# GpSimd computes the low parts of sixteen weight tiles of the latent attention's gate, where VectorE did

## The chip, the cores and the metric

The kernel runs on one core of one Trainium2 chip, as one program. The metric is the device time of one execution in microseconds, taken as the median of several runs.

The core's engines each work through an instruction queue of their own, in order, and wait for each other through semaphores: TensorE (PE in the profile; its weight loads are PEld), VectorE (DVE), ScalarE (ACT), GpSimd (POOL) and SyncE (SP), which only issues transfers here.

## The reference

A stack of three blocks is computed in float32 for one sequence of 256 tokens of width 1024: a retention layer, a latent-attention layer (each followed by a small gated projection), and a block with a convolution, a pooling branch and a feed-forward part. The change touches the latent attention alone:

```python
z = h @ w_in                      # h: (1, 256, 1024)
c_q  = rms_norm(z[..., :768], q_norm_g)
c_kv = rms_norm(z[..., 768:1024], kv_norm_g)
k_rope = rope(z[..., 1024:1088], pos)
gate = z[..., 1088:]              # 2048 columns: 16 heads of 128
...                               # 16 heads of causal attention give o
return (jax.nn.silu(gate) * o) @ w_out
```

The gate's weights are the 2048 last columns of `w_in`, a matrix of 1024 x 2048 numbers.

## The kernel before

**Products in two parts.** A float32 matrix product is made of three products of a shorter format (float32r). Each operand is split into a high part (the operand rounded to that format) and a low part (what is left), and `mm` (L236) issues three matmuls for every 128x128 block of weights: high weights with high activations (L237), high weights with low activations (L238), low weights with high activations (L239). A product by `mm32` (L243) takes the operands whole, in one slower matmul.

**Weight tiles.** Weights arrive as tiles of 128 x 1024 numbers (512 KB), eight blocks of 128x128 in the order of use. `Seq.next` (L148) hands out one block, and calls `load` (L170) at the first block of a tile. `load` fetches the tile to a buffer `raw` (six buffers; the transfer is issued by SP, L165), ScalarE copies it to `wh`, the high part (L178), and VectorE subtracts that from the raw tile to get `wl`, the low part (L179). There are five buffers of `wh` and five of `wl`. A `raw` buffer is free again when both have read it; a `wh` and a `wl` buffer when TensorE has used its last block. So tiles are made ready ahead of TensorE, up to five at a time.

**Order.** The program is written in the order of TensorE's work. A planner puts every engine's instructions into one order when the kernel is built, by that order and by when their inputs should be ready; later that order is fixed. A small clock in the program (`after`, `every`, L203 and L423) delays pieces of work by a number of microseconds of TensorE's work, to give other engines time. One such piece is the modulation of the last block (`ada_steps`, L403): one chunk of 512 KB is fetched by SP, and VectorE multiplies and sums it (L413), every 7.61 us of that clock during this stage.

**The stage of the change.** TensorE's order in the latent attention is: three tiles for the rotary key and the latent key and value; six tiles for the latent query; the gate's products, sixteen tiles, two for each of the eight pairs of heads, by `mla_gate` (L822); and the pairs' projections, by `mla_proj` (L845). They are interleaved: six gate tiles (pairs 0 to 2), projections of pair 0, two gate tiles, projections of pair 1, four gate tiles, projections of pair 2, the last four gate tiles, projections of pair 3, and so on. Between them fall the sums of squares of the latent query (squares on ScalarE at L296, added on VectorE at L300 and L302, summed across partitions by TensorE at L363), from which `lora` (L778) makes the normalised latent query on VectorE and ScalarE (L783 to L793, with L187 and L188 for its two parts); the scores of each pair (L885 to L892); the softmax (L896 to L909 on VectorE, L901 and L902 on ScalarE); and the transposes of its result (L920). The result of a gate product leaves PSUM through VectorE (L831) and ScalarE (L832).

GpSimd does little in this kernel: some clearing of buffers, some transfers, and at the very end two additions (L1432).

The gate's sequence of tiles, which the change names, is made at L820:

```python
    seq_g = Seq(nouter("mla_in", range(16), range(8), 1088))
```

Of the kernel before, what the change touches and what calls it, by code (L numbers as in the profile page):

```python
# [11 lines left out]
F32 = mybir.dt.float32  # L12
# [7 lines left out]
P = 128  # L20
# [61 lines left out]
@with_exitstack  # L82
def tile_kernel(ctx, tc, order, xT, pT, pos, vec, cst, cv, rows, wada, wts, outT):
    nc = tc.nc
    V, A, T = nc.vector, nc.scalar, nc.tensor

    cp = ctx.enter_context(tc.tile_pool(name="cp", bufs=1))
    hp_ = ctx.enter_context(tc.tile_pool(name="half", bufs=14))
# [8 lines left out]
    def nm(s):  # L97
        uid[0] += 1
        return f"{s}_{uid[0]}"
# [7 lines left out]
    class Blk:  # L107

        def __init__(self, nb, dt=F32):
            self.t = [hp_.tile([P, 4, S], dt, tag="half", name=nm("half")) for _ in range((nb + 3) // 4)]  # L110
# [31 lines left out]


    class Seq:
        def __init__(self, entries, width=P, parts=True, ready=()):
            self.e, self.w, self.i, self.parts, self.ready = entries, width, 0, parts, list(ready)

        def next(self):  # L148
            per = D // self.w
            s = self.i % per  # L150
            if s == 0:
                self.h, self.l = load(self.e[self.i:self.i + per], self.w, self.parts, self.ready.pop(0) if self.ready else None)
            self.i += 1
            sl = slice(s * self.w, (s + 1) * self.w)
            return self.h[:, sl], self.l[:, sl]

    def fetch(entries, width, parts=True, step=D, pinned=False):
        g = len(order)
        order.append((width, list(entries)))
        n = len(entries) * width  # L160
        tag, bufs = (("raw", 6), ("wh", 5), ("wl", 5))[0 if parts else [0, 1][g % len([0, 1])]]
        raw = wp.tile([P, D], F32, tag=tag, name=nm("raw"), bufs=bufs)
        for o in range(0, n, step):
            e = min(n, o + step)
            d = nc.sync.dma_start(out=raw[:, o:e], in_=wts[g, :, o:e])  # L165
            if pinned:
                tc.keep_in_program_order(d)
        return raw[:, :n]

    def load(entries, width, parts=True, raw=None):  # L170
        if raw is None:
            raw = fetch(entries, width, parts)
        if not parts:
            return raw, raw
        n = raw.shape[1]
        hi = wp.tile([P, D], F32R, tag="wh", name=nm("wh"), bufs=5)[:, :n]
        lo = wp.tile([P, D], F32R, tag="wl", name=nm("wl"), bufs=5)[:, :n]
        A.copy(hi, raw)  # L178
        V.tensor_sub(lo, raw, hi.bitcast(F32))  # L179
        return hi, lo  # L180

    def nouter(name, ms, kbs, c0=0):
        return [(name, kb * P, c0 + m * P) for m in ms for kb in kbs]
# [247 lines left out]
    def ada():  # L431
        mods["n"] += 1
        next(ada_it, None)
# [383 lines left out]

    sgs = {}

    seq_g = Seq(nouter("mla_in", range(16), range(8), 1088))  # L820

    def mla_gate(p):  # L822

# [277 lines left out]
    def conv():  # L1101
        next(conv_it, None)
# [258 lines left out]

    late = late_steps()
    after(1.12, lambda: every(2.6, 3 * NA + 8, lambda: next(late)))


# [141 lines left out]
```

## Time and profile before

| What | Value |
|---|---|
| median of 3 runs | 845.04 us (843.58 to 845.37) |
| the profiled execution, its time | 842.56 us |
| its span in the profile | 840.8 us |
| TensorE busy | 823.7 us (98%) |
| VectorE busy | 702.4 us (84%) |
| ScalarE busy | 552.7 us (66%) |
| GpSimd busy | 9.9 us (1%) |
| subtractions at L179 | 233, 1222 ns each on average |

A row of a timeline gives the start from the beginning of the span, the duration, the engine, the line, the operation, what is written from what, the shape, and the count where neighbours are joined; what stands in brackets is how long the engine was idle before it and what it waited for. A row of the costliest groups ends with the busy time, the mean of one in ns, and the idle time before. `ps` is a tile in PSUM; the others (`t`, `half`, `raw`, `wh`, `wl`, `adach`, `siluc`) lie in SBUF. Busy time of TensorE includes matmuls that overlap.

### The profile page before, as it was taken

The numbers are of one execution on the slowest core, as the hardware profiler recorded it, in microseconds if no ns is written. First come the engines' busy times: TensorE is split into PE (matmuls) and PEld (weight loads), VectorE is DVE, ScalarE is ACT, GpSimd is POOL, SyncE is SP. The second block draws the span as 40 slices with busy tenths as digits, with TensorE's granted clock in tenths as the row PEclk, the third lists the DMA queues.
The fourth block names the chain that finished last, engine by engine and source line by source line (L and its number), as shares of the span: only waits on it lengthen the run. The fifth ranks groups of instructions, "written<-read, shape, count | busy, mean of one in ns | idle before, by whom it ended". The sixth has DMA issues, their size and how long they took to land.

```text
span 840.8 us, 15768 instructions
## 1 busy us (share of the span) xinstructions
PE 823.7 (98%) x6114; PEld 787.2 (94%) x6114; DVE 702.4 (84%) x1283; ACT 552.7 (66%) x966; POOL 9.9 (1%) x30
## 2 busy tenths in 40 slices
PE   8999999999999999998999999999999999999995
PEld 6989899999999999998999999899998999999885
DVE  6999798988889978688864767899677888889986
ACT  7655565555676787777754867998755576666551
POOL 0000000000000000000000000000000000000001
PEclk9999999999999999999999999999999999999999
DMA  9876567779556647364354355246363455567822
GB/s 333 330 253 221 206 225 273 253 267 323 174 176 249 250 149 255 135 242 150 109 181 176 118 209 176 76 174 196 132 240 113 148 188 191 179 220 252 274 79 76
DMA packets 46634, 167.48 MB, mean 199 GB/s; under 512 B 5216, under 2 KB 5472, under 8 KB 46560
## 3 DMA queue, kind: packets, MB, share of 16 engines
q1 hardware_dynamic: 45936, 164.38, 55.6%
q0 software_dynamic: 624, 2.10, 0.8%
q8 instruction: 48, 0.79, 0.4%
q14 instruction: 26, 0.21, 0.1%
HBM read 165.41 MB, written 1.05 MB: 198 GB/s over the span
## 4 chain that ended last, share of the span: by engine, by line
PE 51%; DVE 2%; ACT 1%; issue 1%; DVEq 0%
PE ps L238 13%; PE ps L237 13%; PE ps L239 13%; PE ps L243 10%; PE ps L341 1%; PE ps L363 0%; DVE wl L179 0%; PE ps L920 0%; PE ps L1170 0%; DVE t L1434 0%; DVE sm L1415 0%; DVE half L690 0%; DVE t L1411 0%; DVE t L1412 0%; PE ps L1407 0%
## 5 line engine op out<-in xcount | busy, mean ns | idle before, releaser
L237 PE MATMUL ps<-half,wh 128*128 128x256 f32 x1504 | 426.2, 284 | 0.0
L238 PE MATMUL ps<-half,wh 128*128 128x256 f32 x1504 | 424.0, 282 | 0.7 <-DVE half L188 0.6
L239 PE MATMUL ps<-half,wl 128*128 128x256 f32 x1504 | 422.2, 281 | 0.0
L178 ACT CAST wh<-raw 128x1024 fp32r<-128x1024 f32 x233 | 243.5, 1049 | 156.9 <-PE ps L238 99.7
L179 DVE TENSOR_TENSOR wl<-raw,wh 128x1024 fp32r<-128x1024 f32 x233 | 283.1, 1222 | 61.4 <-ACT wh L178 59.3
L238 PEld LDWEIGHTS ps<-half,wh 128*128 128x128 f32 x1504 | 283.6, 189 | 2.0 <-DVE half L188 1.1
L237 PEld LDWEIGHTS ps<-half,wh 128*128 128x128 f32 x1504 | 283.1, 188 | 1.1 <-ACT half L187 0.5
L239 PEld LDWEIGHTS ps<-half,wl 128*128 128x128 f32 x1504 | 284.0, 189 | 0.0
L243 PE MATMUL ps<-half,raw 128*128 128x256 f32 (+2 forms) x384 | 84.9, 380 | 0.0
L243 PEld LDWEIGHTS ps<-half,raw 128*128 128x128 f32 x384 | 72.6, 190 | 9.9
L237 PE MATMUL ps<-wh,half 128*128 128x512 f32 (+1 forms) x202 | 72.7, 361 | 1.0 <-ACT wh L178 1.0
L238 PE MATMUL ps<-wl,half 128*128 128x512 f32 (+1 forms) x202 | 71.1, 352 | 0.5 <-DVE wl L179 0.5
L239 PE MATMUL ps<-wh,half 128*128 128x512 f32 (+1 forms) x202 | 71.1, 352 | 0.0
L413 DVE CUSTOM_DVE_ANT_0 adach<-adach,siluc 128x1024 f32<-128x1024 f32 x48 | 58.6, 1222 | 13.8 <-DMA adach<-in_wada 13.8
L1087 ACT ACTIVATE t<-apad,vec 128x256 f32<-128x256 f32 x106 | 44.3, 500 | 0.5 <-DVE half L1088 0.5
L237 PEld LDWEIGHTS ps<-wh,half 128*128 128x128 f32 x202 | 38.0, 188 | 6.8 <-ACT wh L178 1.8
L238 PEld LDWEIGHTS ps<-wl,half 128*128 128x128 f32 x202 | 38.1, 189 | 6.0 <-DVE wl L179 1.0
L239 PEld LDWEIGHTS ps<-wh,half 128*128 128x128 f32 x202 | 38.0, 188 | 5.6
L1088 DVE TENSOR_TENSOR half<-half,t 128x512 f32<-128x512 f32 x53 | 36.6, 690 | 3.7 <-ACT t L1087 1.8
L187 ACT CAST half<-t 128x256 fp32r<-128x256 f32 (+1 forms) x47 | 20.6, 454 | 18.1 <-DVE t L1347 10.9
L188 DVE TENSOR_TENSOR half<-t,half 128x256 fp32r<-128x256 f32 (+1 forms) x47 | 21.8, 485 | 4.0 <-ACT half L187 3.0
L1342 ACT ACTIVATE t<-ps,vec 128x256 f32<-128x256 f32 x38 | 21.0, 557 | 2.0 <-PE ps L239 1.2
(290 smaller groups left out, 905.5 us busy)
## 6 DMA issues: line engine op xcount, KB each, us to landing
raw<-in_wts SPq DMA_DIRECT2D x257, 512.0 KB, 4.1
adach<-in_wada SPq DMA_DIRECT2D x48, 512.0 KB, 5.0
half<-in_xT SPq DMA_DIRECT2D x4, 256.0 KB, 6.0
half<-in_rows POOLq DMA_DIRECT2D x2, 512.0 KB, 4.5
out<-t SPq DMA_DIRECT2D x4, 256.0 KB, 2.0
cst<-in_cst SPq DMA_DIRECT2D x1, 928.0 KB, 10.6
raw<-in_wts SPq DMA_DIRECT2D x2, 256.0 KB, 4.2
siluc<-in_cv SPq DMA_DIRECT2D x1, 512.0 KB, 8.5
```

The source lines that it names most:

```text
L178: A.copy(hi, raw)
L179: V.tensor_sub(lo, raw, hi.bitcast(F32))
L187: A.copy(hi, src)
L188: V.tensor_sub(lo, src, hi.bitcast(F32))
L237: T.matmul(ps, l[0], r[0], start=first, stop=False)
L238: T.matmul(ps, l[0], r[1], start=False, stop=False)
L239: T.matmul(ps, l[1], r[0], start=False, stop=last)
L243: T.matmul(ps, w, r, start=first, stop=last)
L413: V.tensor_tensor_reduce(ch, ch, sc, 1.0, 0.0, MUL, ADD, mod[:, n:n + 1])
L1087: A.activation(t[:, b, :], apad[:, i0 + b, k:k + S], AF.Copy, scale=w[b])
L1088: V.tensor_add(acc.pair(i0 // 2), acc.pair(i0 // 2), t)
L1342: A.activation(t[:, b, :], ps[:, b, :], AF.Identity, bias=col("b_dw_f_2", m), scale=w[2])
```

## The change

`load` and `Seq` get an argument `by` with the engines for the two parts. The gate's sequence passes ScalarE for the high part, as before, and GpSimd for the low part. So sixteen of the 233 subtractions at L179 are issued to GpSimd's queue in place of VectorE's. All other sequences use the default, ScalarE and VectorE. The branch for a high part on GpSimd is not taken by any caller.

```diff
-    V, A, T = nc.vector, nc.scalar, nc.tensor
+    V, A, T, G = nc.vector, nc.scalar, nc.tensor, nc.gpsimd
...
-        def __init__(self, entries, width=P, parts=True, ready=()):
-            self.e, self.w, self.i, self.parts, self.ready = entries, width, 0, parts, list(ready)
+        def __init__(self, entries, width=P, parts=True, ready=(), by=None):
+            self.e, self.w, self.i, self.parts, self.ready, self.by = entries, width, 0, parts, list(ready), by
...
-                self.h, self.l = load(self.e[self.i:self.i + per], self.w, self.parts, self.ready.pop(0) if self.ready else None)
+                self.h, self.l = load(self.e[self.i:self.i + per], self.w, self.parts, self.ready.pop(0) if self.ready else None, self.by)
...
-    def load(entries, width, parts=True, raw=None):
+    def load(entries, width, parts=True, raw=None, by=None):
...
-        A.copy(hi, raw)
-        V.tensor_sub(lo, raw, hi.bitcast(F32))
+        first, second = by or (A, V)
+        if first is G:
+            G.tensor_copy(hi, raw)
+        else:
+            A.copy(hi, raw)
+        second.tensor_sub(lo, raw, hi.bitcast(F32))
...
-    seq_g = Seq(nouter("mla_in", range(16), range(8), 1088))
+    seq_g = Seq(nouter("mla_in", range(16), range(8), 1088), by=(A, G))
```

## Rows read from the trace of the kernel before

**Rows 1.** From the profile page: the first line of busy time, share and instructions by engine; the group of the subtractions at L179; and the group of the tile transfers, with its count, size and median time from issue to landing in us.

```profile
PE 823.7 (98%) x6114; PEld 787.2 (94%) x6114; DVE 702.4 (84%) x1283; ACT 552.7 (66%) x966; POOL 9.9 (1%) x30
...
L179 DVE TENSOR_TENSOR wl<-raw,wh 128x1024 fp32r<-128x1024 f32 x233 | 283.1, 1222 | 61.4 <-ACT wh L178 59.3
...
raw<-in_wts SPq DMA_DIRECT2D x257, 512.0 KB, 4.1
```

**Rows 2.** Busy time in three stretches of the stage of the change: the stretch, its length, then us and instructions of PE, PEld, DVE, ACT and POOL, the granted clock, the DMA share and GB/s. The last row is the same table for line L179 alone, where DVE is the only engine.

```profile
257.00:270.00 13.00, 13.00 (x112) 13.00 (x112) 12.32 (x22) 8.71 (x13) 0.00 (x0) 1.00 0.56 194
...
290.00:310.00 20.00, 19.04 (x158) 18.65 (x157) 14.64 (x39) 15.12 (x30) 0.00 (x0) 1.00 0.43 155
...
330.00:351.00 21.00, 21.00 (x177) 20.87 (x176) 14.80 (x34) 15.07 (x29) 0.00 (x0) 1.00 0.41 142
...
257.00:270.00 13.00, 6.22 (x6) 1.00 0.56 194
```

**Rows 3.** All waits of TensorE from 260 to 350 us (first row) and from 350 to 400 us (the others): who waited for whom, us in total, times, longest.

```profile
PE ps L920 <- DVE sm L909: 1.0, 1, 1.0
...
PE ps L920 <- DVE sm L909: 1.8, 1, 1.8
PE ps L243 <- ACT a L925: 0.7, 1, 0.7
```

**Rows 4.** GpSimd's two additions near the end: the timeline row of the first, then the summary of both (duration min/median/max in ns, start of the first and of the last in us); the same summary of VectorE's products at L1431 and of its operations at L1434, which read two tiles of SBUF.

```profile
831.77 1.73 POOL L1432 TENSOR_TENSOR t<-t,half 128x512 f32<-128x512 f32 x1 [12.68 <-DVE t L1431]
...
L1432 POOL TENSOR_TENSOR t<-t,half x2: 1252/1492/1732, 831.8 to 833.5; 128x512 f32<-128x512 f32 x2
...
L1431 DVE TENSOR_TENSOR t<-t,half x2: 683/688/693, 831.0 to 831.7; 128x512 f32<-128x512 f32 x2
...
L1434 DVE SCALAR_TENSOR_TENSOR t<-t,sm,half x2: 741/759/777, 834.5 to 835.3; 128x512 f32<-128x512 f32 x2
```

**Rows 5.** VectorE's timeline from the first gate tile's subtraction to the sixth's; the four between them and one accumulator read are left out, all else is there.

```profile
257.68 1.23 DVE L179 TENSOR_TENSOR wl<-raw,wh 128x1024 fp32r<-128x1024 f32 x1 [0.58 <-ACT wh L178]
258.83 0.86 DVE L188 TENSOR_TENSOR kr<-t,kr 64x256 fp32r<-64x256 f32 x2
259.72 0.42 DVE L367 TENSOR_TENSOR t<-t 128x256 f32<-128x256 f32 x1
...
261.20 0.42 DVE L372 SCALAR_TENSOR_TENSOR t<-t,t 128x256 f32<-128x256 f32 x1
261.53 1.22 DVE L413 CUSTOM_DVE_ANT_0 adach<-adach,siluc 128x1024 f32<-128x1024 f32 x1
...
262.68 0.42 DVE L373 SCALAR_TENSOR_TENSOR t<-t,t 128x256 f32<-128x256 f32 x1
263.01 0.68 DVE L300 TENSOR_TENSOR t<-t,t 128x512 f32<-128x512 f32 x1
263.62 0.42 DVE L789 TENSOR_TENSOR t<-t,t 128x256 f32<-128x256 f32 x1
...
265.09 0.87 DVE L792 SCALAR_TENSOR_TENSOR t<-ps,gq,t 128x256 f32<-128x256 f32 x2
...
267.01 0.75 DVE L188 TENSOR_TENSOR half<-t,half 128x256 fp32r<-128x256 f32 x2
...
268.81 0.68 DVE L300 TENSOR_TENSOR t<-t,t 128x512 f32<-128x512 f32 x1
269.53 0.43 DVE L302 TENSOR_TENSOR t<-t 128x256 f32<-128x256 f32 x1
269.87 1.22 DVE L179 TENSOR_TENSOR wl<-raw,wh 128x1024 fp32r<-128x1024 f32 x1
```

**Rows 6.** ScalarE's cast of the first gate tile, and from TensorE's timeline the first use of that tile's low part, the sum over the squares of the latent query, and the first use of the sixth gate tile's low part.

```profile
256.60 1.05 ACT L178 CAST wh<-raw 128x1024 fp32r<-128x1024 f32 x1
...
266.16 0.28 PE L239 MATMUL ps<-half,wl 128*128 128x256 f32 x1
...
270.15 0.59 PE L363 MATMUL ps<-t,ones 128*128 128x256 f32 x2
...
280.78 0.28 PE L239 MATMUL ps<-half,wl 128*128 128x256 f32 x1
```

**Rows 7.** Timeline rows around later points: the fetch that follows the first gate tile's subtraction and the cast of the tile it brought; VectorE's low parts of the first pair's keys and values, and the first matmul of its scores; the casts of the ninth and tenth gate tile, and the first use of the ninth's low part; the cast of the last gate tile, and the first use of its low part.

```profile
258.94 0.33 SPq L165 DMA_DIRECT2D raw<-in_wts  x1
...
271.93 1.03 ACT L178 CAST wh<-raw 128x1024 fp32r<-128x1024 f32 x1
...
293.33 1.02 DVE L188 TENSOR_TENSOR t<-ps,t 128x512 fp32r<-128x512 f32 x2
...
295.85 0.28 PE L237 MATMUL ps<-kr,t 128*128 128x256 f32 x1
...
307.94 2.02 ACT L178 CAST wh<-raw 128x1024 fp32r<-128x1024 f32 x2
...
311.61 0.28 PE L239 MATMUL ps<-half,wl 128*128 128x256 f32 x1
...
345.26 1.05 ACT L178 CAST wh<-raw 128x1024 fp32r<-128x1024 f32 x1 [0.41 <-ACT sm L902]
...
348.45 0.40 PE L239 MATMUL ps<-half,wl 128*128 128x256 f32 x2
```

## The prediction

> **What bounds the kernel now.** I began with busy time by engine. TensorE is busy for 823.7 of the 840.8 us of the span and VectorE for 702.4 [rows 1]. That is an average, so next I cut the stage of the change, from 257 us (the first gate tile) to 351 us (the last), into stretches. TensorE is without a gap at the start and at the end; between 290 and 310 us it has 19.04 of 20.00. VectorE is nearly as full at the start, 12.32 of 13.00 from 257 to 270 us, and has room at the end, 14.80 of 21.00 [rows 2]. The waits of TensorE put a price on what a freer VectorE could give back: between 260 and 350 us it waits once, for 1.0 us, for the softmax's last scaling (L909). After 350 us the two waits are 1.8 and 0.7 us [rows 3]. So the stage is bound by TensorE, VectorE close behind it, and a gain is capped at about 1.0 us there. The change can cost more than it can give, if VectorE or the tiles come late.
>
> **What is moved.** Sixteen subtractions of 128x1024 at L179, 1222 ns each on average [rows 1], leave VectorE. Each held its queue for 1.14 us, since the next instruction starts about 0.08 us before it ends. That frees 16 x 1.14 = 18.2 us of VectorE, 5.7 of them with the first five gate tiles, in the full stretch (L179 takes 6.22 us there, gate tiles alone) [rows 2]. The first-part casts on ScalarE, all matmuls and all transfers keep their number.
>
> **What GpSimd pays.** The trace has this kind of operation only at half the size: two 128x512 additions (L1432), 1732 and 1252 ns [rows 4]. Doubling the faster gives 2.50 us as an upper end without disturbance, 1.25 us (no growth) is the lower. VectorE's own two-input operation goes from 688 ns at 512 columns (L1431) to 1222 at 1024 [rows 1, 4], a factor of 1.78; I take 1.25 x 1.78 = 2.22 us. Six gate tiles in a row are needed by TensorE every 2.8 us (first uses of the low part from 266.16 to 280.78 us) [rows 6], so GpSimd alone keeps pace. It can also start early: the first cast ends at 257.65, and the tile is wanted at 266.16 [rows 6]. Six at 2.22 us end at about 271, against a last need of 280.78. Later tiles have less room: the cast of one ends near 308.99 and its low part is used at 311.61 (2.62 us later), that of the last ends at 346.31 and is used at 348.45 (2.14 us) [rows 7]. At 2.22 us that is a stall of 0 and 0.1.
>
> **The queue of transfers.** A raw buffer is released by the subtraction: the fetch at 258.94 us follows the end of the first gate tile's at 258.91 [rows 5, 7]. A later end delays that fetch and the modulation chunks queued behind it on SP. The fetched tile is the sixth after it, cast at 271.93; landing takes 4.1 us [rows 1, 7], so it was there at 263.0 and 8.9 us are spare. Nothing else stands on GpSimd's queue in this stage. I cost this edit at zero; a delay of over 8.9 us would expose it.
>
> **The disputed cost: do the two engines exclude each other?** The first of the two additions on GpSimd started at 831.77, while VectorE ran its second L1431 (from 831.7, 0.69 us long, so until 832.4), and took 0.48 us longer than the second, which had no such neighbour [rows 4]. The excess is about what was left of VectorE's operation (0.6). Both read two operands from SBUF. I read this as one port, held by one of them at a time. It shows GpSimd waiting; no row shows VectorE waiting for GpSimd. The bounds are therefore zero (VectorE never waits) and the whole of each subtraction. I take the whole, because exclusion that is real for one side is most simply mutual, and because whoever comes second finds it taken.
>
> The Trainium skill says the same of the other direction, and speaks against this change: in "SBUF — State Buffer", section "Who interferes with whom", "A DVE instruction with two SBUF inputs contends with a GpSimd instruction that reads SBUF", and the second to issue is blocked until the first finishes. The row agrees for GpSimd as the loser (0.48 us); no run here yet shows VectorE as the loser. By that rule the sum is the one below, while a reading of the row in which only GpSimd waits gives the second rival.
>
> **The sum.** From 257.65 us VectorE's work up to the end of L302 is, without gate tiles: kr parts 0.86, L367 0.42, L372 0.42, L413 1.22, L373 0.42, L300 0.68, L789 0.42, half parts 0.75, L300 0.68, L302 0.43, together 6.30 us, less nine overlaps of 0.08, 5.6 us [rows 5]. All have two SBUF operands; only L792 (0.87) reads PSUM and can run beside GpSimd. Five subtractions fall before L302: 5 x 2.22 = 11.1. One port needs 16.7 us for both, so L302 ends at 274.35. It ended at 269.96, and TensorE used its sum at 270.15 (L363) [rows 5, 6]: 0.19 spare. Late by 274.35 - 269.96 - 0.19 = 4.2 us. TensorE's order is fixed, so everything behind L363 waits too, and a latent chain that follows on VectorE (normalise, split, the query projection) stays as late. The break-even price of a subtraction is (12.31 + 0.19 - 5.6) / 5 = 1.38 us.
> A second place is the first head pair's key split, done at 294.35 and used by the scores from 295.85 [rows 7], 1.5 us spare. Two gate tiles lie before it: 2 x 2.22 of blocking less 2 x 1.14 of relief is 2.2, so 0.7 remains. The last tile's 0.1 is added. The remaining eight lie where VectorE has gaps or reads PSUM, and I give them zero (up to 1.5 in all). Sum: 4.2 + 0.7 + 0.1 = 5.0 us. On the profiled execution that is 842.56 + 5.0 = 847.6. That execution is 2.5 us under the median of the runs (845.04), so the forecast is 850.0 us.
> Its own ends: at 1.25 us a tile nothing is late (845); at 2.50 us L302 is late by 5.6, by 8.1 if the sixth subtraction also gets in ahead of it, and with 2 us for the later groups 10 us, 855.
>
> **The rivals.**
> First, not slower: VectorE never waits for GpSimd, and TensorE's order covers the rest. For it: the 7 to 10 us of lead of the first six tiles, and L1434 on VectorE at 834.50, which started within the second addition (833.50 to 834.72) and took only 0.04 us over its like [rows 4]. That row is weak, as it overlaps only the tail. Price: -0.5 to +0.5, so 845. It decides if a subtraction holds VectorE for under 1.38 us.
> Second, GpSimd alone is the loser: each subtraction is stretched as the first addition was, to 2 x 1.73 = 3.46 us, VectorE runs on. The six still make it (257.65 + 20.8 = 278.4, before 280.78); the tile at 308.99 is late by 0.84 and the last by 1.32: +2.2, 847.2.
> Third, faster: the relief pulls the softmax scaling forward, so that the 1.0 us wait and the 1.8 us one after 350 go: 845.04 - 2.8 = 842.2. Against it: VectorE has gaps before both (14.64 of 20.00 from 290 to 310 us, 14.80 of 21.00 from 330) [rows 2], so it isn't a queue that makes them late, and the gate tiles are over by 350.
>
> **How the numbers follow.** What a measurement of this kernel can tell from no change is about 0.2%, 1.7 us. The forecast gets 0.45, nearly all of it slower. The first rival 0.28, nearly all within 0.2%. The second 0.17, three quarters of it slower. The third 0.10, faster. Slower: 0.44 + 0.13 + 0.01 = 0.58; faster: 0.10 + 0.02 = 0.12; same 0.30. The range goes from 843.0, which leaves out most of the third rival, to 855.0, the upper end of the forecast's bounds. The forecast's own range is 847 to 855.
>
> **What the profile afterwards would show.** Sixteen subtractions on GpSimd near 2.2 us if undisturbed, longer if it waits. If the port is shared as I think, VectorE's two-operand instructions of 0.4 to 1.2 us that meet a subtraction are stretched by up to 2.2 us, while those that read PSUM are not, and TensorE waits for some 4 us at L363 near 270 us. If that wait isn't there and VectorE's durations are unchanged, the first or second rival holds. A wait of TensorE at L239 for the low part from GpSimd speaks for the second. Wrong altogether would be an operation of GpSimd above 5 us, which makes even the first six late, or a re-ordering of TensorE's instructions that covers the lateness with other matmuls.

## The result and the profile after

The changed kernel takes 855.7 us (median of 4 runs, 853.63 to 856.93), the kernel before, with its runs beside them, 844.31 (843.35 to 845.37). The ratio is 1.0135, with a 95% interval from 1.0116 to 1.0155: slower by 11.4 us. The direction was as forecast; the size was not (850.0, range 843.0 to 855.0). The profiled execution took 855.21 us with a span of 853.4 us, 12.65 us more than the profiled one of before, so the steps below add up to 12.65.

The page of the changed kernel (most of its lines stand five lower in the code: the cast is L183, the subtraction L184) shows that the change does what it says [rows 1]:

```profile
PE 829.5 (97%) x6114; PEld 791.7 (93%) x6114; DVE 703.1 (82%) x1267; ACT 551.2 (65%) x966; POOL 50.5 (6%) x46
...
L184 POOL TENSOR_TENSOR wl<-raw,wh 128x1024 fp32r<-128x1024 f32 x16 | 40.5, 2556 | 162.1 <-ACT wh L183 150.4
```

Sixteen subtractions moved, and VectorE is nevertheless as busy as it was. Sixteen times 1.22 us went away, and about as much came back in instructions that last longer. TensorE has the same 6114 matmuls.

All waits of TensorE from 240 to 370 us (who waited for whom, us in total, times, longest) [rows 3]:

```profile
PE ps L368 <- DVE t L307: 5.5, 1, 5.5
PE ps L926 <- DVE sm L915: 3.1, 1, 3.1
PE ps L244 <- POOL wl L184: 0.4, 1, 0.4
```

The first is the wait that the forecast named (the sum of squares, L363 before). The second, for the softmax, was 1.0 us before. For GpSimd's own product TensorE waits 0.4 us in all.

Busy time in stretches, with the granted clock in the third number from the end [rows 2]; of the stretches of 2 us, the first two lie in and behind the first wait, the last behind the second:

```profile
257.00:270.00 13.00, 13.00 (x113) 13.00 (x112) 11.92 (x14) 5.84 (x10) 7.47 (x3) 1.00 0.43 153
270.00:290.00 20.00, 14.45 (x107) 14.06 (x107) 15.56 (x25) 10.52 (x17) 7.59 (x3) 0.83 0.51 184
...
310.00:330.00 20.00, 16.90 (x128) 16.57 (x127) 11.94 (x26) 14.77 (x29) 10.09 (x4) 0.91 0.46 165
...
274.00:276.00 2.00, 0.00 (x0) 0.00 (x1) 1.95 (x1) 0.00 (x0) 2.00 (x2) 0.50 0.65 244
276.00:278.00 2.00, 2.00 (x7) 1.82 (x8) 0.42 (x1) 0.22 (x1) 2.00 (x1) 0.50 0.61 186
...
318.00:320.00 2.00, 2.00 (x12) 2.00 (x11) 1.36 (x5) 2.00 (x5) 1.33 (x1) 0.50 0.35 74
```

From 257 to 270 us VectorE is "busy" for 11.92 us with 14 instructions; before it did 22 in 12.32 [rows 2]. From 274 to 276 TensorE does nothing. When it goes on, its granted clock is 0.50, the lower level (1.2 GHz), and it gets 7 matmuls into 2 us, where 19 are usual. The 12 from 318 to 320 are the same picture behind the second wait.

What VectorE did in that time, and GpSimd beside it (timelines) [rows 5]:

```profile
258.17 5.02 DVE L193 TENSOR_TENSOR kr<-t,kr 64x256 fp32r<-64x256 f32 x2 [0.91 <-ACT kr L192]
263.22 2.52 DVE L372 TENSOR_TENSOR t<-t 128x256 f32<-128x256 f32 x1
265.77 0.43 DVE L377 SCALAR_TENSOR_TENSOR t<-t,t 128x256 f32<-128x256 f32 x1
...
271.96 1.50 DVE L305 TENSOR_TENSOR t<-t,t 128x512 f32<-128x512 f32 x1 [1.65 <-ACT t L301]
273.50 2.44 DVE L307 TENSOR_TENSOR t<-t 128x256 f32<-128x256 f32 x1
277.26 0.42 DVE L789 SCALAR_TENSOR_TENSOR t<-ps,nr 128x256 f32<-128x256 f32 x1 [1.31 <-PE ps L368]
...
298.97 2.60 DVE L765 TENSOR_TENSOR t<-t,t 128x256 f32<-128x256 f32 x1
...
306.39 1.23 DVE L184 TENSOR_TENSOR wl<-raw,wh 128x1024 fp32r<-128x1024 f32 x1 [1.39 <-ACT wh L183]
...
313.18 1.22 DVE L418 CUSTOM_DVE_ANT_0 adach<-adach,siluc 128x1024 f32<-128x1024 f32 x1 [2.60 <-DMA adach<-in_wada]
```

```profile
257.98 7.47 POOL L184 TENSOR_TENSOR wl<-raw,wh 128x1024 fp32r<-128x1024 f32 x3 [100.83 <-ACT wh L183]
270.57 7.59 POOL L184 TENSOR_TENSOR wl<-raw,wh 128x1024 fp32r<-128x1024 f32 x3 [5.13 <-ACT wh L183]
295.45 5.83 POOL L184 TENSOR_TENSOR wl<-raw,wh 128x1024 fp32r<-128x1024 f32 x2 [17.28 <-ACT wh L183]
```

The two instructions for `kr` took 0.86 us before and take 5.02; L372 took 0.42 and takes 2.52 [rows 5]. The three end one after the other with the three subtractions between 257.98 and 265.45, each about 0.3 us behind the end of one. L377 starts when they are over and takes 0.43. L789, which reads PSUM, runs within the second group (270.57 to 278.16) and takes 0.42. So VectorE is held for up to 2.1 us at a time by a subtraction already under way; the held instructions have both of their operands in SBUF, the one that reads PSUM is not held.

Then the queue of transfers: SP's issues (the duration spans the joined issues with the waits between), and SP's waits for subtractions from 255 to 320 us, two rows after the change and one before it [rows 7].

```profile
260.40 15.62 SPq L165 DMA_DIRECT2D raw<-in_wts  x5
276.07 0.42 SPq L411 DMA_DIRECT2D adach<-in_wada  x1
...
307.64 0.33 SPq L165 DMA_DIRECT2D raw<-in_wts  x1
308.02 0.73 SPq L411 DMA_DIRECT2D adach<-in_wada  x1
```

```profile
SPq L165 <- POOL wl L184: 26.4, 8, 7.1
SPq L165 <- DVE wl L184: 9.9, 4, 5.5
...
SPq L165 <- DVE wl L179: 22.0, 10, 5.1
```

SP waits 26.4 us for GpSimd's subtractions to free their raw buffers, but it waited 22.0 us for VectorE's before: it runs ahead and waits in either kernel, so the length of its waits says little. What counts is when a fetch goes out. Before, the chunk of the modulation behind the same five weight fetches went out at 269.30 us; now it goes at 276.07, behind a fetch that waited for GpSimd. The one at 308.02 is the chunk for which VectorE waits 2.60 us ahead of the softmax (L418 at 313.18). It went out at 297.97 before, so it is 10.05 us late where the scores of the first pair are 7.46 us late. The fetch in front of it (307.64) went out 0.02 us after the end of one of VectorE's own subtractions (306.39 to 307.62). By the rows that one was late because VectorE had been held at L765 by GpSimd's second subtraction of the third group, ScalarE had waited 3.87 us for L765, and the cast that the subtraction needs stands behind that on ScalarE. So in this place it is the held VectorE, and not GpSimd's own subtraction, that frees the raw buffer late.

The scores of a pair (first matmul `ps<-kr,t`) serve as marks for the lag, which is how much later than in the kernel before TensorE reaches the same matmul. In the changed kernel, first, second and eighth pair:

```profile
303.31 0.28 PE L242 MATMUL ps<-kr,t 128*128 128x256 f32 x1
...
326.02 0.28 PE L242 MATMUL ps<-kr,t 128*128 128x256 f32 x1
...
433.23 0.28 PE L242 MATMUL ps<-kr,t 128*128 128x256 f32 x1
```

and in the kernel before, second and eighth (the first is in [rows 7]; the fourth pair starts at 377.31 after the change and at 365.44 before):

```profile
315.02 0.28 PE L237 MATMUL ps<-kr,t 128*128 128x256 f32 x1
...
420.60 0.28 PE L237 MATMUL ps<-kr,t 128*128 128x256 f32 x1
```

The lag is 303.31 - 295.85 = 7.46 us at the first pair, then 11.00 at the second, 11.87 at the fourth and 12.63 at the eighth. It comes in two jumps, at the two waits, and 1.6 us trickle in later. At the sum itself the lag is 276.00 - 270.15 = 5.85; the other 1.6 of the first jump is gathered behind it, where TensorE waits for nothing and runs at the lower clock. The second jump is 3.5: 2.1 us more wait at the softmax, and 1.4 behind it.

A lag counts from the beginning of the span, so it also holds what an execution lost ahead of this stage. A mark for that is the previous sum of squares, the last one before the first gate tile: it starts at 252.00 us in the kernel before and at 252.14 after the change (0.14 us of lag), but up to 3.2 us late in the runs below that leave the chunks on SP. Where that matters, the lag from this mark on is given too.

```profile
252.00 0.60 PE L363 MATMUL ps<-t,ones 128*128 128x256 f32 x2
```

### The profile page after: what moved, and what is told of

Its sections match the earlier page's. It is cut to its first block, busy times and chain, and to the rows that moved or that the text cites. A ratio compares the mean times of both kernels' runs of the same rounds, so it can differ in the third digit from the quotient of the medians.

```text
span 853.4 us, 15781 instructions
## 1 busy us (share of the span) xinstructions
PE 829.5 (97%) x6114; PEld 791.7 (93%) x6114; DVE 703.1 (82%) x1267; ACT 551.2 (65%) x966; POOL 50.5 (6%) x46
## 4 chain that ended last, share of the span: by engine, by line
PE 40%; DVE 8%; DMA 3%; issue 2%; ACT 1%; DVEq 0%; SPq 0%; POOLq 0%
PE ps L243 10%; PE ps L242 10%; PE ps L248 10%; PE ps L244 10%; DVE wl L184 2%; DMA adach<-in_wada 1%; DMA g<-mod 1%; PE ps L346 1%; DVE t L1317 1%; DMA half<-g 1%; PE ps L368 0%; DVE t L1349 0%; DVE half L193 0%; DVE t L1350 0%; DVE sm L1421 0%
## 5 line engine op out<-in xcount | busy, mean ns | idle before, releaser
L183 ACT CAST wh<-raw 128x1024 fp32r<-128x1024 f32 x233 | 243.4, 1048 | 147.7 <-PE ps L243 94.2
L184 DVE TENSOR_TENSOR wl<-raw,wh 128x1024 fp32r<-128x1024 f32 x217 | 263.2, 1220 | 57.2 <-ACT wh L183 55.3
L418 DVE CUSTOM_DVE_ANT_0 adach<-adach,siluc 128x1024 f32<-128x1024 f32 x48 | 58.5, 1220 | 15.7 <-DMA adach<-in_wada 15.6
L184 POOL TENSOR_TENSOR wl<-raw,wh 128x1024 fp32r<-128x1024 f32 x16 | 40.5, 2556 | 162.1 <-ACT wh L183 150.4
## 6 DMA issues: line engine op xcount, KB each, us to landing
cst<-in_cst SPq DMA_DIRECT2D x1, 928.0 KB, 10.6
```

Of the source, the lines that this page charges most:

```text
L184: second.tensor_sub(lo, raw, hi.bitcast(F32))
L418: V.tensor_tensor_reduce(ch, ch, sc, 1.0, 0.0, MUL, ADD, mod[:, n:n + 1])
```

## The experiments

Theory A became, in the course of the runs: two causes. GpSimd's subtraction, reading SBUF, holds VectorE's two-operand instructions; and a late subtraction (GpSimd's own, or one of VectorE's behind a held instruction) keeps a raw buffer, so that SP's queue, with the modulation chunk in it, is late and VectorE, in order, waits for the chunk. Both make TensorE stand, and it then runs at the lower clock for some us. Theory B, the rival, has the held VectorE alone.

**Halves of the change.** Low parts on GpSimd for the first six gate tiles only, for the last ten only, and for tiles 8 to 11 only (counted from 0). Of the last the idea was that there GpSimd meets work with PSUM operands.

```diff
-                self.h, self.l = load(..., self.by)
+                self.h, self.l = load(..., self.by if self.i // per < 6 else None)
```

(`>= 6` in the second, `8 <= self.i // per < 12` in the third.)

> Only the first six gate tiles' low parts go to GpSimd, the other ten stay on VectorE. Theory A (GpSimd and VectorE exclude each other while both read two operands from SBUF, in both directions): TensorE waits 5 to 6 us at the sum over the squares of the latent query, then runs some 3 us at the lower clock, and nothing else is lost: 7 to 8 us slower than before, 852. Rival B (the low parts simply come late, VectorE is not held): the six are wanted 7 to 10 us after their casts, so nothing waits, within 1 us of before. Rival C (the planner's new order costs the time, wherever the tiles are computed): a loss without VectorE's instructions being longer.

> The other half: gate tiles seven to sixteen on GpSimd, the first six on VectorE. Theory A: no wait at the sum over the squares, the wait at the transposes of the first pair (3.1 us in the changed kernel against 1.0 before) and the lower clock behind it stay, and so do the small losses at the last tiles: 3 to 6 us slower than before, 848 to 850, so that this and the run with the first six add up to about 12. Rival B: the ninth and the last tile late, 1 to 2 us. Rival C: no forecast.

> Only gate tiles nine to twelve on GpSimd, where VectorE's neighbouring work reads PSUM or has room. Theory A: nothing late, within 1.5 us of before (844), a place without cost but with nothing to gain, since TensorE doesn't wait there. Rival H (each subtraction moved to GpSimd costs its share, wherever it stands): four sixteenths of 11.4 us, 847.

Measured: first six 852.93 us, 1.0096 [1.0075, 1.0117]; last ten 850.12, 1.0068 [1.0053, 1.0083]; four tiles 845.26, 1.0014 [0.9995, 1.0032]. With the first six TensorE waits 5.5 us for the sum, as in the full change, and 1.0 for the softmax, as before; the lag is 7.46 at the first scores and 7.37 at the last. With the last ten there is no wait for the sum, and 3.5 us for the softmax. So the two jumps have separate origins, and the first six tiles carry the larger part. In the run with the first six the second jump is absent; the chunk that goes out at 308.02 in the full change goes out at 305.43 there, 7.46 us later than before, which is just the lag of the scores. The halves add up to 8.1 + 5.7 = 13.8 us (the ratio less one, times the 844.4 us of before), against 11.4. The second wait is 3.1 in the full change, not 3.5; the rest of the difference is not explained, and is about what the intervals of the three runs leave open. The four tiles cost nothing that can be measured, and gain nothing: TensorE has no wait there to give back.

**Hold or absence?** VectorE makes every low part, and GpSimd does the same subtraction once more into the raw tile, which nobody reads afterwards.

```diff
-        second.tensor_sub(lo, raw, hi.bitcast(F32))
+        V.tensor_sub(lo, raw, hi.bitcast(F32))
+        if second is G:
+            G.tensor_sub(raw, raw, hi.bitcast(F32))
```

> VectorE makes all low parts as before, and GpSimd repeats the sixteen subtractions, writing into the raw tile that nobody reads any more. No instruction of TensorE waits for GpSimd's results. Theory A: VectorE is held by the sixteen and not relieved of any: at least as slow as the changed kernel, 856 to 875, with VectorE's two-operand instructions stretched to 2.4 us. Rival B: only the raw and high-part buffers come free later: 844 to 847.

And GpSimd only writes: it clears both tiles before ScalarE and VectorE fill them.

```diff
+        if second is G:
+            G.memset(hi.bitcast(F32), 0.0)
+            G.memset(lo.bitcast(F32), 0.0)
...
-        second.tensor_sub(lo, raw, hi.bitcast(F32))
+        V.tensor_sub(lo, raw, hi.bitcast(F32))
```

> VectorE makes all low parts as before; GpSimd clears the high and the low buffer of each of the sixteen gate tiles before the cast and the subtraction fill them: the same engine, the same places, some 2 us of work per tile that writes SBUF and reads nothing. Theory A (the excluded thing is reading): no VectorE instruction is stretched, within 2 us of before (the cast waits for the clearing, with room for it). Rival D (any work of GpSimd on SBUF holds VectorE, or the semaphores between the three engines cost it): 5 us or more slower, with stretched VectorE instructions.

Measured: doubled 864.77 us, 1.0241 [1.0226, 1.0256]; write-only 847.31, 1.0041 [1.0015, 1.0067]. TensorE's wait for the sum with the doubled work; then, with the clearing, a row of VectorE's timeline and GpSimd beside it:

```profile
PE ps L370 <- DVE t L309: 9.8, 1, 9.8
```

```profile
264.27 0.68 DVE L308 TENSOR_TENSOR t<-t,t 128x512 f32<-128x512 f32 x1
...
264.03 0.95 POOL L184 MEMSET wh<- 128x1024 f32 x1 [0.98 <-PE ps L246]
```

With no relief for VectorE the wait grows from 5.5 to 9.8: the presence of GpSimd's subtraction costs, not the lateness of its product. GpSimd clears for most of 255.59 to 271.55 us, in pairs of 0.95 us each with pauses of 1 us. The addition of the squares (L308, both operands in SBUF) lies wholly inside one clearing and takes 0.68, as before; beside a subtraction, in the changed kernel, it took 1.50 (L305). So GpSimd's writing alone did not hold it. The Trainium skill states this in "SBUF — State Buffer", section "Who interferes with whom": VectorE with two SBUF operands contends with a GpSimd instruction that reads SBUF, "not with one that only writes it". Both halves of that sentence agree with these rows (1.50 us beside a subtraction, 0.68 beside a clearing). The time of this run is 2.9 us above the kernel before, where at most 2 were expected. Nothing of it stands at the sum (271.34 less the mark at 253.19 is 18.15 us, as it was before); it comes later, and what causes it was not separated.

**Shorter holds.** Each of GpSimd's subtractions is cut into four of 256 columns.

```diff
-        second.tensor_sub(lo, raw, hi.bitcast(F32))
+        for o in range(0, n, 256 if second is G else n):
+            e = o + (256 if second is G else n)
+            second.tensor_sub(lo[:, o:e], raw[:, o:e], hi[:, o:e].bitcast(F32))
```

> The changed kernel with each of GpSimd's sixteen subtractions cut into four of 256 columns, some 0.7 us each. Theory A (the two engines take turns, one whole instruction at a time): a held instruction of VectorE then waits for one quarter, so it is stretched by at most 0.8 us where it was 2.1; TensorE's wait at the sum over the squares falls from 5.5 to between 1 and 2.5 us, though GpSimd, held four times as often, may now be late with low parts (a wait of TensorE for the low part of the fourth to sixth gate tile, up to 6 us). In all 847 to 854. Rival E (the two engines share a bandwidth, so that only GpSimd's total reading counts): the same 5.5 us wait and 855 to 857.

Measured: 854.96 us, 1.0121 [1.0099, 1.0143], no measurable gain over whole ones, and above the 847 to 854 expected. The waits of TensorE from 270 to 300 us, and two rows of VectorE's timeline:

```profile
PE ps L244 <- ACT half L194: 2.4, 2, 1.6
PE ps L245 <- DVE half L195: 1.8, 2, 1.1
PE ps L370 <- DVE t L309: 0.3, 1, 0.3
```

```profile
258.11 1.71 DVE L195 TENSOR_TENSOR kr<-t,kr 64x256 fp32r<-64x256 f32 x2 [0.91 <-ACT kr L194]
...
281.86 1.23 DVE L420 CUSTOM_DVE_ANT_0 adach<-adach,siluc 128x1024 f32<-128x1024 f32 x1 [5.41 <-DMA adach<-in_wada]
```

The step itself came out: VectorE is held for some 0.4 us at a time (1.71 for the two `kr` instead of 5.02), and the wait for the sum is 0.3. But the lag at the first scores is 7.45 us, as with whole subtractions. VectorE now stands idle for 5.41 us for a modulation chunk, and the parts of the query, queued behind it, make TensorE wait instead. The reading that made the held VectorE the only cause fell here. So did another rival, that the planner's new order on VectorE makes the sum late: from `kr` up to the sum the order is that of the changed kernel, and the wait is 0.3 us.

**The clock.** Twenty-two small matmuls (44 rows in the profile) on a finished tile, placed before the sum, so that TensorE has something to do while it would wait.

```diff
+        if first == 0:
+            for _ in range(22):
+                T.matmul(pst[:, :P], ones, ones, start=True, stop=True)
```

> The changed kernel with 22 small matmuls of 0.21 us, whose result is overwritten, put in front of the sum over the squares, where TensorE waits for 5.5 us: 4.7 us of work in place of waiting. Theory A with the clock as a cost of its own: the granted clock stays at 1.00 from 270 to 290 us (0.83 in the changed kernel), the rest of the wait is about 1 us, and the 1.6 us that the matmuls at the lower clock cost come back: 854 against 855.7. Rival F (the clock falls for another reason than TensorE's standing still, or costs nothing): 0.83 again and the time unchanged or up.

Measured: 857.44 us, 1.0157 [1.0138, 1.0177]: the time missed the expectation. In the stretch, the dummy matmuls and the sum, and the granted clock where it was 0.50 in the changed kernel, and later:

```profile
L789 PE MATMUL ps<-ones 128*128 128x128 f32 x44 | 5.1, 275 | 0.0
L368 PE MATMUL ps<-t,ones 128*128 128x256 f32 x2 | 0.7, 431 | 0.7 <-DVE t L307 0.7
```

```profile
280.00:282.00 2.00, 2.00 (x19) 2.00 (x19) 0.00 (x0) 0.00 (x0) 1.23 (x1) 1.00 0.93 338
...
304.00:306.00 2.00, 2.00 (x13) 2.00 (x13) 2.00 (x3) 0.00 (x0) 2.00 (x1) 0.65 1.02 406
```

The wait became work of 5.1 us, and the clock stayed at 1.00. From the sum to the first product of the pair's values TensorE needs 21.09 us here (279.04 to 300.13), 20.71 in the kernel before (270.15 to 290.86) and 22.32 after the change (276.00 to 298.32). So 1.2 of the 1.6 us behind the wait are the lower clock, as far as one profile of each kernel can tell. The gain did not show in the time. TensorE stood once more at 302 us, 1.8 us of it waiting for GpSimd's product, and again ran at 0.65 and 0.50 behind it; and this execution was 3.0 us late before the stage began (its `kr` parts start at 261.18, not 258.17).

**The chunk, moved.** With the last ten tiles alone, the modulation's chunks moved 14 us later, then every 6.6 us.

```diff
         mla_proj(p)
+        if p == 0:
+            mods["last"] += 14.0
+            mods["rate"] = 6.6
```

> The run with the last ten tiles on GpSimd, with one modulation chunk of the last block moved behind the softmax of the first pair (the later chunks follow a little closer). Theory A, second place (the raw tile's fetch waits for a subtraction that comes late behind VectorE's held instructions, the chunk's fetch waits behind it on SP, VectorE waits for the chunk and with it the softmax): TensorE's wait at the first pair's transposes falls from 3.5 to 1.5 us or less, the lower clock behind it goes too, and the kernel comes to 846 to 848. Rival G (the softmax is late because VectorE itself is held by GpSimd): 3.5 us again, 850.

Measured: 850.54 us, 1.0071 [1.0054, 1.0089]; the time missed the 846 to 848 expected. The wait for the softmax near 315 us fell from 3.5 to 1.0, and the lag at the fourth pair's scores from 7.30 (last ten alone) to 3.40; from the mark ahead of the stage on it is 5.62 and 2.87. But the moved chunks made new waits behind that: the lag is 6.04 two pairs later and 6.86 at the end, and from the mark on 6.33 at the end in both runs. The place was right, the remedy only moved it.

**The chunk, on a queue of its own.** The chunks go through ScalarE's queue, one ahead: with the change, with quarters, and with the kernel before as control.

```diff
-            tc.keep_in_program_order(nc.sync.dma_start(out=ch, ...))
+            tc.keep_in_program_order(nc.scalar.dma_start(out=ch, ...))
...
-        have = [fetch(0), fetch(1)]
+        have = [fetch(0)]
...
+            if n + 1 < 48:
+                have.append(fetch(n + 1))
             V.tensor_tensor_reduce(ch, ch, sc, 1.0, 0.0, MUL, ADD, mod[:, n:n + 1])
-            if n + 2 < 48:
-                have.append(fetch(n + 2))
```

> The change as it is, but the modulation chunks are fetched through ScalarE's queue (one chunk ahead), so that they don't stand behind weight fetches which wait for GpSimd's tiles. Theory A (two causes: VectorE held by GpSimd makes the latent query's sum late, and a weight fetch held on SP makes the modulation chunk late, with which VectorE's queue waits): the wait for the sum stays at 5 to 5.5 us, the wait for the softmax near 315 us falls from 3.1 to about 1.0 us and the granted clock stays at 1.00 from 310 to 330; 852 us. Theory B (only the held VectorE matters; the chunk stands first in its queue by chance): both waits stay, 855 to 856 us.

> GpSimd's subtractions in quarters and the modulation chunks through ScalarE's queue. Theory A: with whole subtractions replaced by quarters the wait for the sum is gone (0.3 us in the run with quarters), and with its own queue the chunk comes in time, so VectorE's 5.4 us wait for it is gone too: no wait of TensorE over 2 us in the stage, 846 to 849 us. Theory B: 854 to 855 us, as with quarters alone.

> Control: the kernel before (VectorE subtracts), with the modulation chunks through ScalarE's queue. Both theories: within 1.5 us of the kernel before, 843 to 846 us, since no fetch is held by GpSimd there.

Measured: whole subtractions 879.79 us, quarters 869.63, control 869.16. The control missed: the new queue, with one chunk ahead in place of two, costs 25 us without any change to the subtractions, most of it outside this stage (one wait of 8.5 us stands at L341). So the absolute times say nothing, and only the distance to the control does: +10.6 us with whole subtractions, +0.5 with quarters. With quarters and without the chunk on SP, TensorE has no wait over 1.1 us from 240 to 345 us. With whole ones it waits 7.4 us for the sum, where 5 to 5.5 were expected, and 0.8 for the softmax, where about 1.0 was. The first two rows are those of 270 to 310 and of 310 to 345 us with quarters, the third that of 270 to 310 with whole ones:

```profile
PE ps L245 <- DVE half L195: 1.1, 1, 1.1
...
PE ps L246 <- POOL wl L186: 1.1, 1, 1.1
```

```profile
PE ps L368 <- DVE t L307: 7.4, 1, 7.4
```

As this variant changed the whole kernel, the question was put once more with less.

**Two chunks moved, then all of the first 30 us.** With quarters, the chunks 16 us later and every 6.4 us, with a control; then 24 us later and every 5.4 us, with quarters, control, and whole subtractions.

```diff
     mod_rate(7.61)
+    mods["last"] += 16.0
+    mods["rate"] = 6.4
```

> GpSimd's subtractions in quarters, and the modulation chunks of the stage on SP as before but two of them moved from its first 20 us to after 290 us (16 us later, then every 6.4 in place of 7.61 us). Theory A (two causes, the held VectorE and the chunk whose fetch stands behind a held weight fetch): no wait of TensorE over 1.5 us from 270 to 300 us and the granted clock at 1.00 from 284 to 298, where quarters alone had 0.69 and 0.89; the lag at the first pair's scores, 7.45 us with quarters alone, falls to 0 to 2 us; the time is that of its control, the kernel before with the same shift, within 2.5 us. Theory B (with quarters it is still the held VectorE that makes TensorE late): the lag stays at 6 to 8 us, and the time is 6 to 10 us above the control.

> Control: the kernel before (VectorE subtracts) with the same shift of the modulation chunks. Both theories: 0 to 4 us above the kernel before, since chunks that fall later meet the later pairs; no stretched instruction of VectorE.

> GpSimd's subtractions in quarters, and all modulation chunks of the stage moved behind its first 30 us or so (24 us later, then every 5.4 us). In the run with a shift of 16 us one chunk was still fetched at 277.09, behind a weight fetch that waited for GpSimd, and VectorE stood idle for 5.38 us for it; here none is left there. Theory A (held VectorE and held fetch are both causes): no idle time of VectorE over 2 us before a modulation product from 265 to 295, no wait of TensorE over 1.2 us from 270 to 300 us, lag at the first pair's scores 0 to 2 us where it was 7.45 and 7.94, and a time within 3 us of the control with the same shift. Theory B (the held VectorE alone): lag of 6 to 8 us, 6 to 10 us over the control.

> Control: the kernel before with the same shift of 24 us and rate of 5.4. Both theories: 0 to 5 us above the kernel before, since the chunks then meet the later pairs.

> The change with whole subtractions, and the same shift of the chunks. Theory A: the wait for the sum of the latent query is 2.5 to 5.5 us, as one chunk product (1.2 us) fewer stands before it; with the lower granted clock behind it the time is 4 to 9 us above the control, and the softmax near 315 us waits for no chunk. Theory B: 6 to 10 us above the control too; the pair of this run and the run with quarters tells them apart.

Measured: 16 us: quarters 854.15 (1.0118 [1.0092, 1.0144]), control 845.84. 24 us: quarters 854.96 (1.0126 [1.0102, 1.0151]), control 844.27, whole subtractions 857.64 (1.0165 [1.0139, 1.0191]). The shift of 16 left the chunk that mattered in its place (VectorE idle 5.38 us for it), so it missed its aim; its lag of 7.94 (6.67 from the mark on) is about that of quarters alone (7.45 and 7.32). The shift of 24 moved that chunk too. The mark ahead of the stage and the first scores with quarters, in the control, and with whole subtractions, one kernel each:

```profile
252.48 0.60 PE L370 MATMUL ps<-t,ones 128*128 128x256 f32 x2
...
296.55 0.28 PE L244 MATMUL ps<-kr,t 128*128 128x256 f32 x1
```

```profile
254.39 0.60 PE L363 MATMUL ps<-t,ones 128*128 128x256 f32 x2
...
298.24 0.28 PE L237 MATMUL ps<-kr,t 128*128 128x256 f32 x1
```

```profile
252.93 0.60 PE L368 MATMUL ps<-t,ones 128*128 128x256 f32 x2
...
303.35 0.28 PE L242 MATMUL ps<-kr,t 128*128 128x256 f32 x1
```

Against the kernel before (295.85) the lags are 0.70, 2.39 and 7.50 us. The whole 2.39 of the control was there before the stage: at the mark it is 2.39 us late already. From the mark on, the kernel before needs 43.85 us to the first scores; the lags are 0.22, 0.00 and 6.57. With short holds and no chunk in the way, GpSimd's first six tiles cost next to nothing: TensorE has no wait from 230 to 300 us. With whole ones it still waits 4.1 us for the sum. Quarters with the chunk in its place had 7.32. So for the first jump both causes are shown, and each alone is enough for 6 to 7 us (6.57 - 0.22 = 6.35 for the length of the holds, 7.32 - 0.22 = 7.10 for the chunk). One reserve stands: with the chunks moved, the planner also put the key's two instructions later on VectorE, so the second difference holds that too; for the chunk itself speaks VectorE's idle time of 5.41 us. The times did not follow. They are 10.7 us above the control with quarters, where 3 were expected, and 13.4 with whole ones, where 4 to 9 were, because the chunks now stand in the second place. With quarters, TensorE waits there 7.0 us in three waits for the softmax (300 to 350 us), behind VectorE waiting for a chunk:

```profile
305.15 1.23 DVE L420 CUSTOM_DVE_ANT_0 adach<-adach,siluc 128x1024 f32<-128x1024 f32 x1 [4.26 <-DMA adach<-in_wada]
```

With whole subtractions VectorE waits for chunks there too (2.60 and 2.42 us), where none was expected. The control, with the same chunks at the same place and VectorE's subtractions, waits 1.0 us for the softmax there. No version tried beats the kernel before; the four tiles equal it.

## Why the prediction was right in direction and wrong in size

- **"TensorE bounds the stage, VectorE close behind; at most 1.0 us to gain."** Right: the third rival (faster) found nothing, and the four tiles without cost gained nothing.
- **GpSimd's price, 2.22 us.** Measured 2.34 to 2.41 us for undisturbed ones (2.34 in the second group, 2.38, 2.41, 2.39 and 2.37 for the single ones near the end), 2556 ns on average. Undisturbed they are within the bounds; beside VectorE they are longer.
- **The disputed cost.** The exclusion is mutual, as taken; `kr` and L372 show VectorE as the loser, and the first rival (VectorE never waits) fell. The second rival (only GpSimd stretched, to 3.46 us) fell too: one of sixteen reached 3.45 (it began at 297.83, beside a modulation product of VectorE from 297.82 to 299.03), and TensorE waited for GpSimd's product 0.4 us.
- **The first term, 4.2 us at the sum.** The place and the mechanism were right; the wait is 5.5 us. The length of a subtraction was too small: the first three took 7.47 us, the next two 5.06, so five took 12.5 where the forecast has 11.1. With these the forecast's own sum puts the end of L302 (L307 now) at 275.8, and it ended at 275.94. That the fit is so close is in part luck. The forecast lined up work without gaps, but VectorE also stood for 0.91 us (before `kr`, while ScalarE still cast the gate tile and the key) and for 1.65 us (before L305, for ScalarE, which had itself waited 6.97 us for VectorE). Other work must have overlapped by about as much; no run separates the two.
- **The clock, a term that the sum did not have, is one step that failed.** The forecast let TensorE go on at full speed. Behind each long wait it ran at 0.50 of its clock for a few us. That is 1.6 + 1.4 = 3.0 us in two places; of the first, 1.2 were shown by filling the wait, the rest and the second are read from the rows.
- **The queue of transfers, costed at zero, is the other step that failed.** I compared the weight tile's arrival with its cast (8.9 us spare), and named the modulation chunks behind it without asking when they are wanted. The chunk of 269.30 us went out at 276.07, and the one of 308.02 (297.97 before) made VectorE wait 2.60 us in front of the softmax: 2.1 us of extra wait for TensorE. In the first place the same lateness was hidden under the held VectorE, and came out, at full price, when the hold was shortened.
- **The second term, 0.7 us at the first pair's key split**, was nothing: the lag is 7.46 at the value products ahead of the scores and 7.46 at the scores. The two gate tiles that it named did cost time, by the path of the bullet above: they held VectorE at L765 (2.60 us), and the cost came out at the softmax. **The last tiles' 0.1** stand against 0.9 by the fourth pair and 0.8 after that. What these are made of was not separated: from 360 us on TensorE waits 1.9 us for the softmax, 1.0 for ScalarE and 0.4 for GpSimd's product, where it waited 1.8 and 0.7 before.

Sum as measured: 5.85 (at the sum) + 1.6 + 2.1 + 1.4 + 0.9 + 0.8 = 12.65 us, against 4.2 + 0.7 + 0.1 = 5.0. Of the 7.65 us between, 3.0 are the clock and 2.1 the queue, both at nothing in the forecast; the first term was 1.65 too small, of which 0.14 stood before the stage, and the small terms 0.9.

## What to carry to other kernels

An instruction moved to an idle engine is paid for by all whom it holds. In this kernel that was GpSimd's whole length for each instruction of VectorE that had both operands in SBUF and met a subtraction, so cost it so, and then follow each buffer that it frees later through the queue behind it, up to the last one who wants something from that queue. When a long wait goes away and the time stays, look for the next queue that was late under its cover. A wait of TensorE can cost more than its length: here 1.2 us of lower clock came behind one of 5.5.

## What the runs showed of the hardware

VectorE was held at the level of single instructions: in the first group one two-operand instruction of VectorE got through for each of GpSimd's subtractions, however small. A 128x8 addition (L423) took 2.37 us where it took 0.17 before. An instruction with one SBUF tile and a per-partition scalar, also in SBUF, was held as well: the two softmax scalings of 128x128 took 2.69 us at 357.21, where they take 0.55 otherwise.

```profile
295.53 2.37 DVE L423 TENSOR_TENSOR mod<-mod,vec 128x8 f32<-128x8 f32 x1
```

GpSimd's subtractions of a quarter size took 0.72 to 0.74 us undisturbed, so four are 2.9 us where a whole one is 2.4: cutting costs half a us per tile and shortens the hold by 1.7.
